# A fifth kind of expert for up to 32 tokens, and another order of the branches, in a two-layer decoder trunk

## The chip, the core and the metric

The kernel runs on one core of one Trainium2 chip. The metric is the device time of one execution in microseconds (us). The kernel before was timed three times; a profiled execution of it, with the trace that is read here, is a fourth. TensorE is PE in the rows (PEld its weight loads, PEldq and PEq its sequencer), VectorE is DVE, ScalarE ACT, GpSimd POOL, SyncE SP. MiB is 1,048,576 bytes.

## What is computed

The reference is two decoder layers on 256 tokens of 1024 channels. Only the last part matters here: in the second layer the channel mixer is a top-2-of-8 mixture of experts. Each expert is a SwiGLU with two 1024 x 2816 matrices and one 2816 x 1024 matrix in float32:

```python
def _moe(h, w_router, b_router, w1, w3, w2):
    t = h.reshape(-1, d)
    logits = (t @ w_router + b_router).astype(jnp.float32)
    top_val, top_idx = lax.top_k(logits, TOP_K)
    top_w = jax.nn.softmax(top_val, axis=-1)
    gates = jnp.sum(jax.nn.one_hot(top_idx, N_EXPERTS, dtype=jnp.float32) * top_w[..., None], axis=1)
    out = jnp.zeros_like(t)
    for e in range(N_EXPERTS):
        out = out + gates[:, e:e + 1].astype(t.dtype) * _swiglu(t, w1[e], w3[e], w2[e])
    return out.reshape(bsz, seq, d)
```

With the inputs that are timed, the reference sends 20, 54, 194, 113, 23, 40, 43 and 25 tokens to experts 0 to 7 (512 in all). The kernel computes only the tokens that an expert has.

## The kernel before, in words

Everything up to the router runs once in a fixed order. `moe` (L1098) then goes through the eight experts in order (L1417). The router counts each expert's tokens and turns the count into a number `ov` by three comparisons on DVE (L1049 to L1051): 0 for up to 64 tokens, 1 for up to 128, 2 for up to 208 (`MANY`), 3 above. For each expert all five engines load that number into a register (L1418) and take one of four bodies through nested branches (L1426 to L1435): `small` (L1168), `middle` (L1245), `many` with 208 slots, `many` with 256. In the program each branch is followed by the body of its true side, then by its false side; after a body the engine jumps to the point where the next expert's number is loaded. So `small` is entered without a jump, `middle` with one, `many` at 208 with two; and each body but the last one placed ends in a jump.

Weights. Each expert's weights are 33 parts of 1 MiB: 11 blocks, each of two parts of w1 and w3 (`w13m`) and one part of w2. They go through a ring of 15 buffers (L1091 to L1094), in one order for all eight experts (`parts`, L1085 to L1090), 264 parts in all. `refill` (L178) issues on SP every part that the ring has room for; the program calls it after each stage, and each issue waits on SP until PE has read the buffer's last part. `moe_begin` fills the ring once (L1095), during the end of the layer before.

`small` works on one 128 x 128 array of PE as two column groups of 64 columns (`tile_position=(0, 64 * h)`), each with the expert's 64 token slots as its stationary operand. It gathers the tokens from `hn` by a 0/1 matrix (L1175, the channels' halves in the two groups, 512 columns each), copies them out of PSUM on ACT and DVE (L1178, L1179), transposes them (L1183) and adds the shift (L1187). `stage1` (L1195) runs, for each block and each of 8 chunks of the contraction, one matmul per group over 256 columns of weights (L1200): w1's columns in the first group, w3's in the second. SiLU is on ACT (L1204), the product on DVE (L1205). `stage2` (L1208) transposes the product (L1212), copies it (L1215) and accumulates 512 columns of the output in each group (L1218). The groups' results are in two PSUM banks. The order is stage1(0), stage1(1), stage2(0), stage1(2), and so on; after the last block the rows are scaled (L1234), scattered back to the tokens by matmuls (L1240) and added to `x_t` on DVE (L1141). For the last expert each chunk of channels also goes through the final norm (`finish`, L1145), and four DMAs write the output (L1166).

A float32 matmul is two LDWEIGHTS and two MATMUL records in the trace; some records of a trace can be missing.

An expert of kind `middle` or `many` splits the weights into two parts on ACT and DVE (`load_parts`, L210 and L211) and multiplies with the whole array.

Of the kernel before, what the change touches and what calls it, by code (L numbers as in the profile page):

```python
# [9 lines left out]
F32 = mybir.dt.float32  # L10
# [4 lines left out]
AF = mybir.ActivationFunctionType  # L15
ALU = mybir.AluOpType
# [19 lines left out]
P = 128  # L36
D = 1024
KC = 8
T = 256
# [4 lines left out]
NB = 11  # L44
# [47 lines left out]
def trunk_kernel(ctx: ExitStack, tc: tile.TileContext, xT, sm, co, w_ada0, w_ada, w_in, w_v, s5bc, w_glu,  # L92
# [12 lines left out]
    def nm(s):  # L105
        cnt[0] += 1
        return f"{s}_{cnt[0]}"
# [990 lines left out]
    def moe():  # L1098
# [66 lines left out]
                for q in range(2):  # L1165
                    nc.sync.dma_start(out[tb * P:(tb + 1) * P, 512 * q:512 * q + 512], o[:, q, :])  # L1166

        def small(e):  # L1168

            pm = pms[e % 2]  # L1170
            hf = (slice(0, 64), slice(64, 128))
            ps = [mm_ps("xg") for _ in range(2)]
            for tb in range(2):
                for h in range(2):
                    PE.matmul(ps[h][hf[h], :], lhsT=pm[:, tb, 0:64], rhs=hn[:, tb, 512 * h:512 * h + 512],  # L1175
                              start=tb == 0, stop=tb == 1, tile_position=(0, 64 * h))
            xs = mo.tile([P, 512], F32, name=nm("xs"), tag="pt", bufs=2)
            S.activation(xs[hf[0]], ps[0][hf[0], :], AF.Copy)  # L1178
            V.tensor_copy(xs[hf[1]], ps[1][hf[1], :])  # L1179
            ps = mm_ps("xg")  # L1180
            xe = lp.tile([P, KC * 64], F32, name=nm("xs"), tag="hh")
            for c in range(4):
                PE.transpose(ps[:, c * P:(c + 1) * P], xs[:, c * P:(c + 1) * P], ident)  # L1183

            xe4, ps4 = (t.rearrange("p (c h s) -> p h c s", c=4, h=2) for t in (xe, ps))
            for h in range(2):
                V.tensor_tensor(xe4[:, h], ps4[:, h], sh[:, 4 * h:4 * h + 4].unsqueeze(2).broadcast_to([P, 4, 64]), op=ALU.add)  # L1187
            y = [ms_ps("y", 0) for _ in range(2)]

            def rows_of(src, rows, cols):  # L1190
                n = min(rows, 2048 // cols)
                return [w[:, r, :] for i in range(0, rows, n)
                        for w in (load_raw(src[:, i:i + n, :], n, cols),) for r in range(n)]

            def stage1(j):  # L1195
                w = rows_of(w13m[e, j], KC, 512)
                ps = [mm_ps("s1") for _ in range(2)]
                for k in range(KC):
                    for h in range(2):
# [3 lines left out]
                sg = mo.tile([P, 256], F32, name=nm("sg"), tag="pt", bufs=2)  # L1203
                S.activation(sg[hf[1]], ps[0][hf[0], 0:256], AF.Silu)  # L1204
                V.tensor_tensor(sg[hf[1]], sg[hf[1]], ps[1][hf[1], 0:256], op=ALU.mult)  # L1205
                return sg

            def stage2(j, sg):  # L1208
                w = rows_of(w2m[e, j], 2, 1024)
                ps = ms_ps("gT", 1)  # L1210
                for k in range(2):
                    PE.transpose(ps[:, k * 64:(k + 1) * 64], sg[hf[1], k * P:(k + 1) * P], ident[hf[1], hf[1]],  # L1212
                                 tile_position=(64, 0))
                g = mo.tile([P, 2, 64], F32, name=nm("gT"), tag="gT", bufs=2)
                S.activation(g, ps[:, 0:P].rearrange("p (k s) -> p k s", k=2), AF.Copy)  # L1215
                for k in range(2):
                    for h in range(2):
                        PE.matmul(y[h][hf[h], :], lhsT=g[:, k, :], rhs=w[k][:, 512 * h:512 * h + 512],  # L1218
                                  start=j == 0 and k == 0, stop=j == NB - 1 and k == 1, tile_position=(0, 64 * h))
                refill()  # L1220

            prev = None
            for j in range(NB):
                sg = stage1(j)
                if prev is not None:
                    stage2(j - 1, prev)
                prev = sg
                if j == 1:
                    ahead(e)
                    ge, gs = back_of(e, 64)  # L1230
            stage2(NB - 1, prev)
            ys = lp.tile([P, 512], F32, name=nm("ys"), tag="hh")
            for h in range(2):
                S.activation(ys[hf[h]], y[h][hf[h], :], AF.Copy, scale=gs[hf[h]])  # L1234
            gf = ge.bitcast(F32)
            fin.update(n=0, a=ms_ps)
            for c in range(4):
                ps = [mm_ps("sc") for _ in range(2)]
                for h in range(2):
                    PE.matmul(ps[h][:, 0:T], lhsT=ys[hf[h], c * P:(c + 1) * P], rhs=gf[hf[h], :],  # L1240
                              start=True, stop=True, tile_position=(64 * h, 0))
                for h in range(2):
                    add_back(e, 4 * h + c, ps[h][:, 0:T])

        def middle(e):  # L1245

# [168 lines left out]
                    add_back(e, 2 * q + i, ps[:, i * T:(i + 1) * T])  # L1415

        for e in range(NE):  # L1417
            rv = nc.values_load(ov[0:1, e:e + 1], engines=ENGS, min_val=0, max_val=3,  # L1418
                                skip_runtime_bounds_check_because="it is a sum of three comparisons")
# [194 lines left out]
```

## Time and profile before

| what | us |
|---|---|
| median of three runs | 1573.48 |
| lowest and highest of them | 1571.73 and 1580.18 |
| the profiled execution, its own time | 1569.24 |
| its span, first to last instruction | 1567.5 |
| experts 0 to 7 in it (from the first gather) | 744.7 to 1567.5 |

The span is what the trace shows, and all positions are counted from its start; 1.7 us of the execution's time lie around it. The first 744 us are the part that the change does not touch. In the experts' part the kinds follow one another as small, small, many (208), middle, small, small, small, small.

How to read it: the two engines that matter are PE and the DMA queue that brings the weights. Where the DMA share is 1 the 16 DMA engines are never idle and the weights set the pace; where it is well below, the ring is full and an engine sets the pace. A taken branch shows as a COMPARE_BRANCH record whose length is the time that the sequencer stood at it.

### The profile page before, as it was taken

How to read it: one execution, taken by the hardware profiler on the slowest of the kernel's cores; microseconds unless marked ns; L12 is line 12 of the kernel's file. 1: busy time of each engine (PE TensorE's matmuls, PEld its weight loads, DVE VectorE, ACT ScalarE, POOL GpSimd, SP SyncE). 2: the span in 40 equal slices, each digit the busy share in tenths (PEclk: the TensorE clock that was granted, in tenths of full speed). 3: DMA queues.
4: the chain of work that ended last, by engine and by line, in shares of the span. 5: the costliest groups of instructions: out<-in, count | busy, mean ns of one | idle time of the engine just before them, and what ended most of it. 6: DMA issues, size and time to landing. Idle time of an engine off the chain costs nothing.

```text
span 1567.5 us, 24755 instructions
## 1 busy us (share of the span) xinstructions
PE 1371.7 (88%) x9903; PEld 1139.8 (73%) x9903; DVE 881.6 (56%) x1443; ACT 605.2 (39%) x1115; POOL 318.9 (20%) x295
## 2 busy tenths in 40 slices
PE   4788999799998878988998949999799897979796
PEld 3676998699997777988665648988677574747474
DVE  7888679897777778687111036666588301010102
ACT  3453564354455534644111125555477211111112
POOL 0568019986201625050000000000000000000000
PEclk8898999799999899999998969999899998989899
DMA  7454356477776344479899975666399599999993
GB/s 285 174 190 160 125 188 212 136 258 240 261 257 223 133 136 135 166 244 403 359 419 416 419 290 189 215 203 203 130 348 351 212 420 416 419 416 419 417 419 122
DMA packets 60379, 420.37 MB, mean 268 GB/s; under 512 B 6688, under 2 KB 6688, under 8 KB 11296
## 3 DMA queue, kind: packets, MB, share of 16 engines
q1 hardware_dynamic: 56160, 403.34, 67.9%
q0 software_dynamic: 4032, 14.68, 2.8%
q8 instruction: 100, 1.64, 0.4%
q14 instruction: 87, 0.71, 0.1%
HBM read 416.94 MB, written 1.05 MB: 267 GB/s over the span
## 4 chain that ended last, share of the span: by engine, by line
PE 70%; DVE 18%; issue 6%; DMA 2%; ACT 2%; DVEq 0%; SPq 0%; ACTq 0%
PE s L1200 16%; PE mm L231 15%; PE y L1218 8%; DVE wl L211 6%; PE s L1350 4%; PE y L1372 4%; PE facc L971 3%; PE s L1267 3%; PE s L1352 2%; PE y L1286 2%; DMA raw<-in_w13m_dram 2%; DVE acc L309 1%; PE mm L716 1%; PE xg L1175 1%; DVE x_t L1141 1%
## 5 line engine op out<-in xcount | busy, mean ns | idle before, releaser
L211 DVE TENSOR_TENSOR wl<-raw,wh 128x1024 fp32r<-128x1024 f32 (+1 forms) x290 | 391.0, 1363 | 118.6 <-ACT wh L210 116.2
L210 ACT ACTIVATE wh<-raw 128x1024 fp32r<-128x1024 f32 (+1 forms) x290 | 302.3, 1057 | 252.1 <-PE mm L231 102.1
L231 PE MATMUL mm<-hh,wh 128*128 128x256 f32 x864 | 250.7, 292 | 5.1 <-ACT hh L250 2.9
L231 PE MATMUL mm<-hh,wl 128*128 128x256 f32 x864 | 249.7, 290 | 5.8 <-DVE wl L211 5.8
L1200 PE MATMUL s<-raw,xs 128*64 128x256 f32 x1920 | 250.1, 390 | 3.4 <-DVE xs L1187 3.4
L231 PE MATMUL mm<-hl,wh 128*128 128x256 f32 x864 | 249.5, 289 | 2.0 <-DVE hl L251 1.0
L1200 PEld LDWEIGHTS s<-raw,xs 128*64 128x64 f32 x1920 | 183.8, 140 | 48.2 <-issue 13.9
L1205 DVE TENSOR_TENSOR sg<-sg,s 64x256 f32<-64x256 f32 x66 | 28.0, 424 | 318.6 <-ACT sg L1204 269.8
L231 PEld LDWEIGHTS mm<-hh,wl 128*128 128x128 f32 x864 | 169.4, 196 | 9.8 <-DVE wl L211 6.3
L231 PEld LDWEIGHTS mm<-hh,wh 128*128 128x128 f32 x864 | 169.0, 196 | 9.4 <-ACT hh L250 3.3
L231 PEld LDWEIGHTS mm<-hl,wh 128*128 128x128 f32 x864 | 169.2, 196 | 3.7 <-DVE hl L409 1.5
L1218 PE MATMUL y<-raw,gT 128*64 128x512 f32 x520 | 143.1, 600 | 4.7 <-ACT gT L1215 4.7
L1204 ACT ACTIVATE sg<-s 64x256 f32<-64x256 f32 x66 | 24.8, 375 | 314.2 <-PE s L1200 314.2
L1350 PE MATMUL s<-xe,wh 128*128 128x416 f32 x352 | 107.2, 368 | 2.0 <-DVE sg L1360 1.7
L1352 PE MATMUL s<-xe,wl 128*128 128x208 f32 x352 | 91.0, 258 | 0.0
L309 DVE SCALAR_TENSOR_TENSOR acc<-raw,cond,acc 128x512 f32<-128x512 f32 x91 | 81.4, 894 | 1.6
L1218 PEld LDWEIGHTS y<-raw,gT 128*64 128x64 f32 x520 | 51.1, 136 | 40.9 <-issue 30.5
L317 POOL TENSOR_TENSOR araw<-araw,cond 128x1024 f32<-128x1024 f32 x28 | 62.3, 2229 | 71.8 <-DMA araw<-in_w_ada_dram 71.8
L1350 PEld LDWEIGHTS s<-xe,wh 128*128 128x128 f32 x352 | 66.2, 188 | 4.3 <-DVE sg L1360 2.4
L1352 PEld LDWEIGHTS s<-xe,wl 128*128 128x128 f32 x352 | 67.3, 191 | 0.4
L971 PE MATMUL facc<-fgh,wh 128*128 128x256 f32 x352 | 62.9, 281 | 0.2 <-ACT wh L210 0.2
L321 POOL TENSOR_TENSOR araw<-araw,araw 128x1024 f32<-128x1024 f32 x21 | 58.2, 2773 | 1.6
(513 smaller groups left out, 2369.0 us busy)
## 6 DMA issues: line engine op xcount, KB each, us to landing
raw<-in_w13m_dram SPq DMA_DIRECT2D x160, 1024.0 KB, 13.8
raw<-in_w2m_dram SPq DMA_DIRECT2D x87, 1024.0 KB, 13.7
raw<-in_w_ada_dram SPq DMA_DIRECT2D x32, 1024.0 KB, 5.1
raw<-in_w_in_dram SPq DMA_DIRECT2D x28, 1024.0 KB, 5.0
raw<-in_w13d_dram SPq DMA_DIRECT2D x22, 1024.0 KB, 5.0
late<-in_w13m_dram SPq DMA_DIRECT2D x16, 1024.0 KB, 16.2
araw<-in_w_ada_dram POOLq DMA_DIRECT2D x28, 512.0 KB, 4.6
raw<-in_w2d_dram SPq DMA_DIRECT2D x11, 1024.0 KB, 5.0
```

The costliest lines, as they stand in the source:

```text
L210: S.activation(hv, rv, AF.Copy)
L211: V.tensor_tensor(lv, rv, hv.bitcast(F32), op=ALU.subtract)
L231: PE.matmul(ps, lhsT=a[k][:, c0:c0 + P], rhs=b[:, k, :], start=k == 0 and i == 0 and o % 2 == 0, stop=k == n - 1 and i == 2 and o % 2 == 1)
L309: V.scalar_tensor_tensor(acc0, raw[:, k, :], c, acc0, op0=ALU.mult, op1=ALU.add)
L317: G.tensor_tensor(raw, raw, cond[:, r0:r0 + 2].unsqueeze(2).broadcast_to([P, 2, 512]), op=ALU.mult)
L321: G.tensor_tensor(acc, acc, raw, op=ALU.add)
L971: PE.matmul(o, lhsT=a[k][:, oc * P:(oc + 1) * P], rhs=b[:, k, :], start=j == 0 and oc % 2 == 0 and k == 0 and i == 0, stop=j == NB - 1 and ...
L1200: PE.matmul(ps[h][hf[h], 0:256], lhsT=xe4[:, k // 4, k % 4, :], rhs=w[k][:, 256 * h:256 * h + 256], start=k == 0, stop=k == KC - 1, tile_p ...
L1218: PE.matmul(y[h][hf[h], :], lhsT=g[:, k, :], rhs=w[k][:, 512 * h:512 * h + 512], start=j == 0 and k == 0, stop=j == NB - 1 and k == 1, til ...
L1350: PE.matmul(ps[:, 0:2 * nb], lhsT=hs[k][:, c], rhs=x.rearrange("p i s -> p (i s)"), start=k == 0, stop=False)
L1352: PE.matmul(ps[:, nb:2 * nb], lhsT=ls[k][:, c], rhs=x[:, 0, :], start=False, stop=k == KC - 1)
L1372: PE.matmul(y[b][n][0:s1 - s0, :], lhsT=g[:, k, s0:s1], rhs=w[w_][k][:, n * 512:n * 512 + 512], start=j == 0 and k == 0 and i == 0, stop=j ...
```

## The change

It adds a fifth kind. The comparison with 32 makes `ov` run from 0 to 4. `small(e, n)` now takes 32 or 64 slots: with n = 32 it uses four column groups of 32 columns (`G_ = 4`), each with a quarter of the weights' columns (128 in `stage1`, 256 in `stage2` and in the gather), so the number of matmuls doubles and each is half as wide. In both sizes the groups' results now lie in one PSUM bank instead of two, and the final scaling is one ACT instruction on 128 partitions instead of two on 64. The branches are nested anew, and three of them ask for the false side to be placed next (`preferred_fallthrough_block=False`).

```diff
-        V.tensor_scalar(o64, ps[:, 16:24], 64.0, None, op0=ALU.is_gt)
-        V.scalar_tensor_tensor(o64, ps[:, 16:24], float(P), o64, op0=ALU.is_gt, op1=ALU.add)
+        V.tensor_scalar(o64, ps[:, 16:24], 32.0, None, op0=ALU.is_gt)
+        for n in (64, P):
+            V.scalar_tensor_tensor(o64, ps[:, 16:24], float(n), o64, op0=ALU.is_gt, op1=ALU.add)
...
-        def small(e):
+        def small(e, n):
...
+            G_ = P // n
+            cb = KC // G_
+            gr = [slice(n * g, n * g + n) for g in range(G_)]
+            lo, hi = slice(0, 64), slice(64, 128)
+            w_ = D // G_
+            ps = mm_ps("xg")
             for tb in range(2):
...
+                for g in range(G_):
+                    PE.matmul(ps[gr[g], 0:w_], lhsT=pm[:, tb, 0:n], rhs=hn[:, tb, w_ * g:w_ * g + w_],
+                              start=tb == 0, stop=tb == 1, tile_position=(0, n * g))
...
-                ps = [mm_ps("s1") for _ in range(2)]
+                ps = mm_ps("s1")
+                c_ = 512 // G_
                 for k in range(KC):
-                    for h in range(2):
-                        PE.matmul(ps[h][hf[h], 0:256], lhsT=xe4[:, k // 4, k % 4, :], rhs=w[k][:, 256 * h:256 * h + 256],
-                                  start=k == 0, stop=k == KC - 1, tile_position=(0, 64 * h))
+                    for g in range(G_):
+                        PE.matmul(ps[gr[g], 0:c_], lhsT=xe4[:, k // cb, k % cb, :], rhs=w[k][:, c_ * g:c_ * g + c_],
+                                  start=k == 0, stop=k == KC - 1, tile_position=(0, n * g))
...
+                for k in range(2 * n // 64):
+                    PE.transpose(ps[:, k * 64:(k + 1) * 64], sg[hi, k * P:(k + 1) * P], ident[hi, hi], tile_position=(64, 0))
...
-                    for h in range(2):
-                        PE.matmul(y[h][hf[h], :], lhsT=g[:, k, :], rhs=w[k][:, 512 * h:512 * h + 512],
-                                  start=j == 0 and k == 0, stop=j == NB - 1 and k == 1, tile_position=(0, 64 * h))
+                    for h in range(G_):
+                        PE.matmul(y[gr[h], 0:w_], lhsT=g[:, k, :], rhs=w[k][:, w_ * h:w_ * h + w_],
+                                  start=j == 0 and k == 0, stop=j == NB - 1 and k == 1, tile_position=(0, n * h))
...
-            with tc.If(rv < 1) as c:
-                arm(small)
+
+            with tc.If(rv < 2, preferred_fallthrough_block=False) as c:
+                with tc.If(rv < 1, preferred_fallthrough_block=False) as c1:
+                    arm(lambda e: small(e, 32))
+                with c1.Else():
+                    arm(lambda e: small(e, 64))
             with c.Else():
-                with tc.If(rv < 2) as c2:
+                with tc.If(rv < 3, preferred_fallthrough_block=False) as c2:
                     arm(middle)
                 with c2.Else():
-                    with tc.If(rv < 3) as c3:
+                    with tc.If(rv < 4) as c3:
                         arm(lambda e: many(e, MANY))
```

Experts 0, 4 and 7 (20, 23 and 25 tokens) become the new kind; 1, 5 and 6 stay `small` with 64 slots.

## Rows read from the trace of the kernel before

**Rows 1.** The page's 40 slices of the span: DMA share and GB/s.

```profile
DMA  7454356477776344479899975666399599999993
GB/s 285 174 190 160 125 188 212 136 258 240 261 257 223 133 136 135 166 244 403 359 419 416 419 290 189 215 203 203 130 348 351 212 420 416 419 416 419 417 419 122
```

**Rows 2.** By stretch, experts 0, 2, 3, 6: length, busy per engine, PEclk, DMA share, GB/s.

```profile
726.00:827.00 101.00, 85.54 (x630) 60.73 (x628) 24.09 (x91) 18.51 (x49) 0.00 (x0) 0.93 0.96 396
...
909.00:1117.00 208.00, 183.45 (x1080) 164.66 (x1080) 122.49 (x185) 102.86 (x168) 0.00 (x0) 0.94 0.58 197
1117.00:1231.00 114.00, 106.88 (x474) 83.98 (x474) 91.65 (x102) 73.69 (x89) 0.00 (x0) 0.97 0.82 305
...
1394.00:1476.00 82.00, 72.75 (x506) 47.92 (x506) 10.12 (x25) 9.51 (x26) 0.00 (x0) 0.94 1.01 418
```

**Rows 3.** Short stretches: around expert 4's start, in expert 6, at the end.

```profile
1230.00:1240.00 10.00, 6.33 (x32) 2.72 (x34) 2.73 (x8) 0.59 (x1) 0.00 (x0) 0.83 0.01 2
...
1394.00:1400.00 6.00, 4.77 (x12) 1.57 (x12) 1.23 (x4) 0.59 (x1) 0.00 (x0) 0.50 1.01 410
...
1410.00:1420.00 10.00, 10.00 (x80) 6.91 (x78) 0.58 (x2) 1.03 (x3) 0.00 (x0) 1.00 1.01 421
...
1540.00:1542.00 2.00, 2.00 (x21) 1.86 (x19) 0.00 (x0) 0.00 (x0) 0.00 (x0) 1.00 0.04 16
```

**Rows 4.** Timeline of SP: first refill of expert 0, of expert 4, last weight issues.

```profile
754.81 0.33 SPq L183 DMA_DIRECT2D raw<-in_w13m_dram  x1
...
1239.96 0.33 SPq L183 DMA_DIRECT2D raw<-in_w13m_dram  x1
...
1519.55 2.81 SPq L183 DMA_DIRECT2D raw<-in_w2m_dram  x2
```

**Rows 5.** The chain in order of time: last stage2 and gathers (start, us, what).

```profile
815.34 1.99 PE y L1218 x8
...
827.38 3.70 PE xg L1175 x8
...
897.52 1.99 PE y L1218 x8
...
924.14 7.68 PE xg L1333 x48
...
1232.22 3.61 PE xg L1175 x8
...
1546.38 1.99 PE y L1218 x8
```

**Rows 6.** Branches by line and short stretch: ns min/median/max, first and last start.

```profile
L1426 PEldq COMPARE_BRANCH  x1: 95/95/95, 744.4 to 744.4; - x1
...
L1426 PEldq COMPARE_BRANCH  x2: 77/3108/6138, 820.5 to 827.1; - x2
...
L1426 PEldq COMPARE_BRANCH  x2: 5971/6575/7179, 902.7 to 909.1; - x2
...
L1429 PEldq COMPARE_BRANCH  x1: 7396/7396/7396, 916.5 to 916.5; - x1
...
L1426 PEldq COMPARE_BRANCH  x1: 4356/4356/4356, 1113.1 to 1113.1; - x1
...
L1429 PEldq COMPARE_BRANCH  x1: 3958/3958/3958, 1227.5 to 1227.5; - x1
...
L1426 SPq COMPARE_BRANCH  x2: 38/44/50, 906.7 to 907.5; - x2
...
L1429 SPq COMPARE_BRANCH  x1: 50/50/50, 912.2 to 912.2; - x1
```

**Rows 7.** Timeline of PE: four column groups (L282) and two (L1200).

```profile
28.80 1.07 PE L282 MATMUL adar<-raw,condr 128*32 128x256 f32 x16
...
1237.90 3.67 PE L1200 MATMUL s<-raw,xs 128*64 128x256 f32 x32 [0.57 <-DVE xs L1187]
```

**Rows 8.** Timeline of DVE in the router: one comparison of the counts.

```profile
743.15 0.17 DVE L1050 SCALAR_TENSOR_TENSOR rlg<-rank,rlg 128x8 f32<-128x8 f32 x1
```

More of the change, by code (lines that the diff above doesn't have):

```diff
@@ L1166, in finish @@
                     nc.sync.dma_start(out[tb * P:(tb + 1) * P, 512 * q:512 * q + 512], o[:, q, :])
-        def small(e):
+        def small(e, n):
             pm = pms[e % 2]
-            hf = (slice(0, 64), slice(64, 128))
-            ps = [mm_ps("xg") for _ in range(2)]
-            for tb in range(2):
-                for h in range(2):
[L1175 to L1179, printed above, removed]
+            G_ = P // n
[4 more added lines that the diff above has]
+            ps = mm_ps("xg")
+            for tb in range(2):
+                for g in range(G_):
+                    PE.matmul(ps[gr[g], 0:w_], lhsT=pm[:, tb, 0:n], rhs=hn[:, tb, w_ * g:w_ * g + w_],
+                              start=tb == 0, stop=tb == 1, tile_position=(0, n * g))
+            xs = mo.tile([P, w_], F32, name=nm("xs"), tag="pt", bufs=2)
+            S.activation(xs[lo], ps[lo, 0:w_], AF.Copy)
+            V.tensor_copy(xs[hi], ps[hi, 0:w_])
@@ L1180, in small @@
             ps = mm_ps("xg")
-            xe = lp.tile([P, KC * 64], F32, name=nm("xs"), tag="hh")
-            for c in range(4):
+            xe = lp.tile([P, KC * n], F32, name=nm("xe"), tag="hh")
+            for c in range(cb):
                 PE.transpose(ps[:, c * P:(c + 1) * P], xs[:, c * P:(c + 1) * P], ident)
-            xe4, ps4 = (t.rearrange("p (c h s) -> p h c s", c=4, h=2) for t in (xe, ps))
-            for h in range(2):
-                V.tensor_tensor(xe4[:, h], ps4[:, h], sh[:, 4 * h:4 * h + 4].unsqueeze(2).broadcast_to([P, 4, 64]), op=ALU.add)
@@ L1188, in small @@
-            y = [ms_ps("y", 0) for _ in range(2)]
+            xe4, ps4 = (t[:, 0:KC * n].rearrange("p (c g s) -> p g c s", c=cb, g=G_) for t in (xe, ps))
+            for g in range(G_):
+                V.tensor_tensor(xe4[:, g], ps4[:, g], sh[:, cb * g:cb * g + cb].unsqueeze(2).broadcast_to([P, cb, n]),
+                                op=ALU.add)
+            y = ms_ps("y", 0)
             def rows_of(src, rows, cols):
-                n = min(rows, 2048 // cols)
-                return [w[:, r, :] for i in range(0, rows, n)
-                        for w in (load_raw(src[:, i:i + n, :], n, cols),) for r in range(n)]
+                m = min(rows, 2048 // cols)
+                return [w[:, r, :] for i in range(0, rows, m)
+                        for w in (load_raw(src[:, i:i + m, :], m, cols),) for r in range(m)]
@@ L1195, in stage1 @@
             def stage1(j):
                 w = rows_of(w13m[e, j], KC, 512)
-                ps = [mm_ps("s1") for _ in range(2)]
+                ps = mm_ps("s1")
+                c_ = 512 // G_
                 for k in range(KC):
-                    for h in range(2):
-                        PE.matmul(ps[h][hf[h], 0:256], lhsT=xe4[:, k // 4, k % 4, :], rhs=w[k][:, 256 * h:256 * h + 256],
-                                  start=k == 0, stop=k == KC - 1, tile_position=(0, 64 * h))
+                    for g in range(G_):
+                        PE.matmul(ps[gr[g], 0:c_], lhsT=xe4[:, k // cb, k % cb, :], rhs=w[k][:, c_ * g:c_ * g + c_],
+                                  start=k == 0, stop=k == KC - 1, tile_position=(0, n * g))
@@ L1210, in stage2 @@
                 ps = ms_ps("gT", 1)
+                for k in range(2 * n // 64):
+                    PE.transpose(ps[:, k * 64:(k + 1) * 64], sg[hi, k * P:(k + 1) * P], ident[hi, hi], tile_position=(64, 0))
+                g = mo.tile([P, 2, n], F32, name=nm("gT"), tag="gT", bufs=2)
+                S.activation(g, ps[:, 0:2 * n].rearrange("p (k s) -> p k s", k=2), AF.Copy)
                 for k in range(2):
[L1212 to L1217, printed above, removed]
-                        PE.matmul(y[h][hf[h], :], lhsT=g[:, k, :], rhs=w[k][:, 512 * h:512 * h + 512],
-                                  start=j == 0 and k == 0, stop=j == NB - 1 and k == 1, tile_position=(0, 64 * h))
+                    for h in range(G_):
+                        PE.matmul(y[gr[h], 0:w_], lhsT=g[:, k, :], rhs=w[k][:, w_ * h:w_ * h + w_],
+                                  start=j == 0 and k == 0, stop=j == NB - 1 and k == 1, tile_position=(0, n * h))
                 refill()
@@ L1229, in small @@
                     ahead(e)
-                    ge, gs = back_of(e, 64)
+                    ge, gs = back_of(e, n)
             stage2(NB - 1, prev)
-            ys = lp.tile([P, 512], F32, name=nm("ys"), tag="hh")
-            for h in range(2):
-                S.activation(ys[hf[h]], y[h][hf[h], :], AF.Copy, scale=gs[hf[h]])
+            ys = lp.tile([P, w_], F32, name=nm("ys"), tag="hh")
+            S.activation(ys, y[:, 0:w_], AF.Copy, scale=gs)
             gf = ge.bitcast(F32)
             fin.update(n=0, a=ms_ps)
[L1237 to L1243, printed above, removed]
+            for c in range(cb):
+                ps = [mm_ps("sc") for _ in range(G_)]
+                for g in range(G_):
+                    PE.matmul(ps[g][:, 0:T], lhsT=ys[gr[g], c * P:(c + 1) * P], rhs=gf[gr[g], :],
+                              start=True, stop=True, tile_position=(n * g, 0))
+                for g in range(G_):
+                    add_back(e, cb * g + c, ps[g][:, 0:T])
         def middle(e):
@@ L1417, in moe @@
         for e in range(NE):
-            rv = nc.values_load(ov[0:1, e:e + 1], engines=ENGS, min_val=0, max_val=3,
-                                skip_runtime_bounds_check_because="it is a sum of three comparisons")
+            rv = nc.values_load(ov[0:1, e:e + 1], engines=ENGS, min_val=0, max_val=4,
+                                skip_runtime_bounds_check_because="it is a sum of four comparisons")
             def arm(f):
```

6 lines of the change are left out of this document (3 added, 3 removed).

## The prediction

> **What bounds the kernel now.** First the page's slices: the DMA share stands at 9 from slice 18 to 23 and again near the end, at 400 to 420 GB/s [rows 1]. Only the experts' part is changed, so the second view is one row per expert. Expert 6 (64 slots) holds the DMA engines at share 1.01 and 418 GB/s for all of its 82 us; expert 0 is at 0.96; expert 2 (208 slots) at 0.58 and expert 3 (128 slots) at 0.82 are bound by PE and the engines that feed it [rows 2]. At 418 GB/s a part of 1 MiB takes 2.51 us, an expert's 33 parts 82.8 us: as long as PE spends on a small expert. Both limits lie on one another, and a faster PE alone can gain only what the ring has in stock.
>
> So I count when the DMA queue stops and starts. It starts again with the first refill of an expert that found the ring full: 754.8 in expert 0, 1240.0 in expert 4 [rows 4]; just before the latter the share is 0.01 [rows 3]. From 1240.0, experts 4 to 7 need 132 - 15 = 117 more parts, 293.7 us; the last bytes come at about 1541.5 [rows 3], 301.5 us after the first refill, since the engines finish unevenly. PE ends its last stage2 at 1546.38 + 1.99 = 1548.4 [rows 5], 19.1 us before the end.
>
> The third view is the branches [rows 6]. One not taken costs PE under 0.1 us. One taken with the weight queue busy costs 5.97 to 7.40 us, with the queue idle 3.96 to 4.36. Between experts 1 and 2 PE takes three: the exit and two on the way to `many`.
>
> **The change, step by step.** I call the branches A (rv < 2), B (rv < 1), C (rv < 3). With the false side next, `many` at 208 is entered without a jump, `middle` by C, `small` with 64 by A, with 32 by A and B. The body with 32 lies last, so I give it no exit jump; the others keep theirs. For a taken branch I use 7.0 us with the queue busy (entries 7.18 and 7.40, exits nearer 6) and 4.2 idle [rows 6].
>
> *Matmuls.* Four groups of 32 columns run in the trace already: 16 records of 256 columns in 1.07 us, four steps; two groups of 64 take 3.67 us for 32 records, 16 steps [rows 7]. The 12 steps between them are 2.60 us, 0.217 each, and a tail of 0.4 is left: four records side by side cost what two cost. At 128 columns I take half a step, 0.108. A block of the new body then needs 16 x 0.108 + 4 x 0.217 = 2.6 us of matmuls and about 0.5 around them, against 16 x 0.217 + 4 x 0.43 + 0.5 = 5.7 before. The DMA queue needs 7.5 us per block. The new body waits for weights once the ring is empty.
>
> *Expert 0.* The extra comparison is 0.2 us [rows 8]. PE's branch at 744.4 was not taken [rows 6]; now A and B are, +14.0 (bounds: 8.4 if the ring has filled by then, 14.8). In return gather, transposes and the first part of stage1 are half as long, about 4 us of the 10.4 between branch and first refill (bounds 0 and 5.5). First refill 754.8 + 0.2 + 14 - 4 = 765. The queue is idle until then, so this is paid in full. The expert's last part is 18 refills later: 765 + 45.2 + 2.5 (landing) + 1.5 = 814 for the end of its stage2, against 815.34 + 1.99 = 817.3 [rows 5].
>
> *Expert 1.* Before, 3.2 us lay between that end and the branch at 820.5, and 6.9 to the gather at 827.4, of which 6.1 was the exit branch [rows 5, 6]. Now: 814 + 3.2 + 0.7 + 7.1 (A taken, B not) = 825.0. Its PE time, gather to last stage2, was 899.5 - 827.4 = 72.1 [rows 5], so 897.1; by the weights it is 765 + 51 x 2.51 + 4.5 = 897.5. I take 897.5: 2 us ahead.
>
> *Expert 2.* Two taken branches (7.18 + 7.40) become two not taken, -14.4 [rows 6]. Its gather, at 924.1 before [rows 5], comes 16 us ahead. Experts 2 and 3 stay PE-bound [rows 2], and between them one entry is taken as before: still 16.
>
> *Expert 4.* The way in had no jump; now A and B with the queue idle, +8.4 (14.8 if they cost what they do under load). Its gather (1232.2 before [rows 5]) is 7.6 ahead; half the gather and half the first stage1 part save another 3.4 of the 7.7 us to the first refill (bounds 0 and 4). First refill 1229, 11 us ahead.
>
> *Experts 4 to 7.* The queue needs the same 301.5 us, if it never stops. It stops if PE enters expert 7 too late. From 1229, by the same steps: expert 4 ends its stage2 at 49.2, expert 5 at 132.5, expert 6 at 149.6 + 72.1 = 221.7; then 3.2 + 0.7 + 6.1 (exit) + 14 (A, B) and 4.3 to the first refill give 250. The ring then holds work for the queue up to 99 x 2.51 + 2.5 = 251. With a microsecond or two until new bytes flow I count 1.5 us idle (bounds 0 and 6). SP takes the same branches, 4.7 us for one (907.5 to 912.2 [rows 6]); it is covered, since the last weights issued at about 1522 [rows 4] land 20 us later, and that much is in flight when SP jumps. POOL has no work in an expert. ACT and DVE branch beside PE, and I count PE.
>
> *The end.* Last bytes at 1229 + 301.5 + 1.5 = 1532; PE has then only the last stage2 to do, 1.5 us with its copy, where before it ended 6.9 after the last bytes. One scaling instruction instead of two saves 0.7 of the last 19.1 us: 1532 + 1.5 + 18.4 = 1551.9.
>
> The sum is -15.6 us on the span: of it -2 in experts 0 and 1, -14.4 before expert 2, +8.4 - 3.4 at expert 4, -4.6 at the end, rounded. The profiled execution's own 1569.24 becomes 1553.6. It was 4.2 us under the median of the runs; from the median 1573.48 I come to **1558**.
>
> [...]
>
> [...]
>
> **The rivals.**
>
> *Branches dearer than seen* (slower). The new body has about twice the PE instructions, and a taken branch into it may cost more than any row. Each extra microsecond counts three times before expert 1's end (A, B, A) and four times before expert 7's first refill (A, A, A, B), once the 1.5 us of slack there are gone. At 12 us per branch: -15.6 + 15 + 20 = +19, 1593. It passes +0.5% from about 10.4 us. Against it: no row is above 7.40.
>
> *The gain is eaten* (no difference). 7.4 at every entry, no quicker first refills (the copies and additions around the half-length matmuls are not halved) and 6 us of idle queue at expert 7: -15.6 + 4.8 + 3.4 + 4.5 = -2.9, 1571.
>
> *The order of the branches does not change.* Then 32 slots enter without a jump and `many` keeps two. Expert 0 refills at 754.8 and ends at 804, expert 1 at 893 (6 ahead), expert 4 refills 9.8 ahead, and the end falls at 1551.6 of the span: 1558, the same number by another way.
>
> *One PSUM bank serialises the groups* (slower). Then 64 slots lose 5.2 us a block, 57 an expert; three experts, some of it inside the weights' time: about 1710. The four-group row writes one bank and runs at 0.217 a step [rows 7].
>
> *PE was the bound.* If PE's 2.6 us per block came off fully, 3 experts x 11 x 2.6 = 85: 1488. The DMA share of 1.01 [rows 2] forbids it.
>
> [...]
>
> **How the numbers follow.** About 0.5%, or 8 us, is what a measurement here can tell from no change. The forecast has 0.58, the order unchanged 0.05, PE as the bound 0.01: faster 0.64. Eaten gain 0.25: same 0.25. Dearer branches 0.09 and serialised groups 0.02: slower 0.11. The range: 8.4 for expert 0's entry, no idle at expert 7 and the best refills give 1549; above it takes in the eaten gain with the clock's 1.4 and a little more, 1574. What is left out are the dear branches, the bank and PE as the bound.
>
> **What would show it.** Right: A and B as two long records at expert 0, the DMA share down to zero between about 757 and 765; expert 2's gather near 908; expert 4's first refill near 1229; PE waiting for weights in experts 0, 4 and 7; the last bytes near 1532 and the end 20 us later. Wrong: a taken branch over 10 us; the two-group matmuls no longer 0.217 a step; PE not waiting for weights with 32 slots; a long idle stretch of the queue before expert 7; a jump on the way to `many`.

## The result, and the profile after

The changed kernel takes 1582.44 us (median of 20 runs, 1575.28 to 1596.67), the kernel before 1571.93 (20 runs, 1564.14 to 1583.3). The ratio is 1.0072, with a 95% interval of 1.005 to 1.0094: the change made the kernel slower by 0.7%. I had predicted 1558 and faster; 1582 lies above the range too.

The profiled execution has a span of 1579.8 us against 1567.5. First the page's slices, which answer to [rows 1]:

```profile
PEclk9798999899998999999768989999899788989796
DMA  7454455477775434569699995655598499999993
GB/s 291 165 198 148 134 185 202 147 260 243 273 256 197 161 103 152 184 227 415 270 417 414 419 367 201 213 202 172 189 355 338 169 418 412 419 405 420 392 373 154
```

The queue is full in the same parts as before. What differs is when it starts and stops. PE's branches (rows of one line and stretch: engine, count, ns min/median/max, first and last start), which answer to [rows 6]:

```profile
L1433 PEldq COMPARE_BRANCH  x1: 6142/6142/6142, 746.3 to 746.3; - x1
L1434 PEldq COMPARE_BRANCH  x1: 4772/4772/4772, 752.5 to 752.5; - x1
...
L1434 PEldq COMPARE_BRANCH  x1: 5910/5910/5910, 820.3 to 820.3; - x1
...
L1433 PEldq COMPARE_BRANCH  x1: 7127/7127/7127, 826.7 to 826.7; - x1
...
L1439 PEldq COMPARE_BRANCH  x1: 3427/3427/3427, 1226.3 to 1226.3; - x1
...
L1434 PEldq COMPARE_BRANCH  x1: 6066/6066/6066, 1299.9 to 1299.9; - x1
...
L1434 PEldq COMPARE_BRANCH  x2: 6267/6928/7588, 1476.1 to 1489.8; - x2
```

Expert 0 is entered by A and B, 10.9 us together. The third row is one that the prediction does not have: the body with 32 slots is left at 820.3 by a jump of 5.91 us, and at 1299.9 (expert 4) by one of 6.07. The body with 128 slots too is left by a jump, at 1226.3 (expert 3), and so is the one with 208, at 1107.4 for 3.49 us. The last row holds two at expert 7: the exit of expert 6 and the entry by B. Only PE's records have the length of the wait: on DVE a branch that is taken has a record as short as one that is not (47 ns for its jump out of expert 1, 43 for the first at expert 2, which is not taken), and the wait stands behind it.

The first refills on SP of experts 0, 4 and 7 (start, length), which answer to [rows 4]:

```profile
765.39 0.33 SPq L183 DMA_DIRECT2D raw<-in_w13m_dram  x1
...
1246.66 0.33 SPq L183 DMA_DIRECT2D raw<-in_w13m_dram  x1
...
1504.18 0.33 SPq L183 DMA_DIRECT2D raw<-in_w13m_dram  x1
```

Before, they were at 754.81 and 1239.96. Short stretches (length, busy per engine with counts, PEclk, DMA share, GB/s), which answer to [rows 3]:

```profile
756.00:765.00 9.00, 5.02 (x60) 3.15 (x61) 4.45 (x28) 1.66 (x2) 0.00 (x0) 0.50 0.01 3
1228.00:1240.00 12.00, 0.00 (x0) 0.00 (x0) 1.99 (x6) 0.00 (x0) 0.00 (x0) 0.64 0.06 10
1495.00:1507.00 12.00, 8.26 (x151) 6.08 (x151) 1.34 (x6) 0.65 (x2) 0.00 (x0) 0.60 0.60 225
...
1545.00:1557.00 12.00, 7.68 (x114) 4.13 (x114) 0.58 (x2) 0.98 (x4) 0.00 (x0) 0.78 0.60 247
1560.00:1570.00 10.00, 9.75 (x30) 5.36 (x30) 4.80 (x12) 5.83 (x16) 0.00 (x0) 0.50 0.00 1
```

The queue is idle before expert 0's first refill, as predicted, and again around expert 7's, with a share of 0.60 over 12 us. At the end PE is granted 0.50. In the kernel before, the stretch behind the last stage2 was at 1.00:

```profile
1548.00:1558.00 10.00, 8.08 (x42) 4.85 (x40) 6.13 (x17) 7.44 (x18) 0.00 (x0) 1.00 0.01 2
```

In the chain in order of time, the rows that answer to [rows 5]:

```profile
794.52 20.11 DMA raw<-in_w2m_dram
...
814.76 1.99 PE y L1225 x16
...
834.09 1.94 PE xg L1180 x3
...
1535.48 19.88 DMA raw<-in_w2m_dram
...
1555.49 1.83 PE y L1225 x16
```

Expert 0 now waits for weights: its last stage2 starts 0.1 us after a transfer has landed. It ends at 816.7 instead of 817.3, but expert 1's gather comes at 834.1 instead of 827.4. The gap between was 10.1 us and is 17.3. The last transfer lands at 1555.4 (before 1541.9; its last bytes were there at 1541.5), and from the end of the last stage2 to the end of the span there are 22.5 us instead of 19.1.

At expert 2, PE takes no jump, as predicted, and starts its gather at 916.5. There it stops. The timelines of DVE and of PE (start, busy time, line, operation; in brackets the idle time before it and what ended it):

```profile
916.70 0.48 DVE L1120 TENSOR_SCALAR pm<-co_t,rrk 128x128 f32<-128x128 f32 x2 [5.49 <-issue]
917.09 0.16 DVE L1329 TENSOR_SCALAR r<-rrk 128x2 f32<-128x2 f32 x1
921.44 0.48 DVE L1332 TENSOR_SCALAR pml<-co_t,r 128x128 f32<-128x128 f32 x2 [4.18 <-issue]
```

```profile
916.52 1.20 PE L1339 MATMUL xg<-pm,late 128*128 128x128 f32 x4 [6.13 <-issue]
921.78 1.15 PE L1339 MATMUL xg<-pml,late 128*128 128x80 f32 x4 [4.06 <-DVE pml L1332]
```

The second block of the gather needs `pml`, which DVE makes at 921.4, after 4.18 us in which it waited for nothing that the profile shows, behind its own jump out of expert 1's body. So the gather goes on at 921.8; before it began at 924.1.

### The profile page after: what moved, and what is told of

It reads as the page before. It is cut to its first block, busy times and chain, and to the rows that moved or that the text cites. A ratio compares the mean times of both kernels' runs of the same rounds, so it can differ in the third digit from the quotient of the medians.

```text
span 1579.8 us, 27425 instructions
## 1 busy us (share of the span) xinstructions
PE 1309.9 (83%) x11256; PEld 1113.0 (70%) x11256; DVE 875.8 (55%) x1450; ACT 595.2 (38%) x1109; POOL 318.4 (20%) x295
## 4 chain that ended last, share of the span: by engine, by line
PE 62%; DVE 17%; issue 9%; DMA 8%; ACT 2%; DVEq 0%; ACTq 0%; SPq 0%
PE mm L231 15%; PE s L1207 10%; PE y L1225 5%; DVE wl L211 5%; PE s L1356 4%; PE y L1378 4%; PE facc L971 3%; DMA raw<-in_w13m_dram 3%; PE s L1273 3%; DMA raw<-in_w2m_dram 3%; PE s L1358 2%; PE y L1292 2%; DVE acc L309 2%; PE mm L716 1%; DMA late<-in_w2m_dram 1%
## 5 line engine op out<-in xcount | busy, mean ns | idle before, releaser
L211 DVE TENSOR_TENSOR wl<-raw,wh 128x1024 fp32r<-128x1024 f32 (+1 forms) x290 | 387.0, 1348 | 120.0 <-ACT wh L210 117.4
L1207 PE MATMUL s<-raw,xe 128*32 128x128 f32 (+1 forms) x2880 | 202.8, 326 | 15.8 <-DMA raw<-in_w13m_dram 12.4
L1207 PEld LDWEIGHTS s<-raw,xe 128*32 128x32 f32 (+1 forms) x2880 | 158.3, 124 | 43.9 <-DMA raw<-in_w13m_dram 17.1
L1212 DVE TENSOR_TENSOR sg<-sg,s 64x128 f32<-64x128 f32 (+1 forms) x66 | 23.6, 358 | 294.3 <-ACT sg L1211 294.3
L1211 ACT ACTIVATE sg<-s 64x128 f32<-64x128 f32 (+1 forms) x66 | 21.3, 323 | 269.8 <-PE s L1207 269.8
L1225 PE MATMUL y<-raw,gT 128*32 128x256 f32 (+1 forms) x776 | 112.9, 488 | 8.9 <-DMA raw<-in_w2m_dram 4.2
L1180 PE MATMUL xg<-late,pm 128*32 128x256 f32 (+1 forms) x72 | 16.5, 770 | 84.9 <-issue 84.9
L1225 PEld LDWEIGHTS y<-raw,gT 128*32 128x32 f32 (+1 forms) x776 | 44.6, 124 | 36.6 <-issue 13.0
L1180 PEld LDWEIGHTS xg<-late,pm 128*32 128x32 f32 (+1 forms) x72 | 4.6, 178 | 92.0 <-issue 92.0
L1358 PEld LDWEIGHTS s<-xe,wl 128*128 128x128 f32 x352 | 67.2, 191 | 0.4
## 6 DMA issues: line engine op xcount, KB each, us to landing
raw<-in_w2m_dram SPq DMA_DIRECT2D x87, 1024.0 KB, 18.7
```

Source lines behind the costliest of these rows:

```text
L211: V.tensor_tensor(lv, rv, hv.bitcast(F32), op=ALU.subtract)
L1207: PE.matmul(ps[gr[g], 0:c_], lhsT=xe4[:, k // cb, k % cb, :], rhs=w[k][:, c_ * g:c_ * g + c_], start=k == 0, stop=k == KC - 1, tile_positi ...
L1225: PE.matmul(y[gr[h], 0:w_], lhsT=g[:, k, :], rhs=w[k][:, w_ * h:w_ * h + w_], start=j == 0 and k == 0, stop=j == NB - 1 and k == 1, tile_p ...
L1358: PE.matmul(ps[:, nb:2 * nb], lhsT=ls[k][:, c], rhs=x[:, 0, :], start=False, stop=k == KC - 1)
```

## The experiments

My theory after the result (J in the expectations) was that the jumps decide: the body with 32 slots is a gain, and the entries and above all its exit cost more than it brings. The rivals were that four column groups cost more than they bring (G), that a program of five bodies is slower to fetch in any order (F), and, for the end alone, that the starved PE falls to half clock (H) or that the work behind this body does so by itself (T).

The part ahead of the router is the same in all these kernels, but its length differs by execution: PE's first branch starts between 740 and 757 us in the profiled ones (744.4 before, 746.3 after), with a granted clock of 0.85 to 0.95 in the stretch from 600 to 700 us. So I give positions **from that branch** as well: the kernel before ends at 823.0 by it, the changed one at 833.4.

**The body taken out, the branches kept**

```diff
-                    arm(lambda e: small(e, 32))
+                    arm(lambda e: small(e, 64))
```

> The changed kernel with one thing undone: up to 32 tokens go through the same five-way branches into the same place, but the body there works with 64 slots on two column groups. Theory J (the loss is PE's taken branches, and the new body itself is a gain): expert 0 refills first near 769, its last stage2 ends near 832, expert 1 gathers near 849 and expert 2 near 936. From expert 4's gather near 1255 four bodies of 72.4 and gaps of 17.3, 17.3 and 24.5 give 1604 for the last stage2 and 1623 for the span, a ratio of 1.035 to the kernel before. Rival G (the body with four groups is what costs: it starves and its end is at half clock): no slower than the changed kernel, 1.000 to 1.007, and the part after the last stage2 is 19 us again instead of 22.5.

Measured: ratio 1.035 (1.0321 to 1.0378). Expert 0's last stage2 ends at 837.7, expert 1 gathers at 854.8 and expert 4 at 1260.1 in an execution whose first branch is 7.6 us later than in the changed kernel; the end is 873.9 from the branch. Rival G falls: behind the new branches four column groups are worth 40 us. The time behind the last stage2 is 18.7 us here, so 3.8 us of the 22.5 do come with the body.

**The order of the branches as before, with the new body**

```diff
-            with tc.If(rv < 2, preferred_fallthrough_block=False) as c:
-                with tc.If(rv < 1, preferred_fallthrough_block=False) as c1:
+            with tc.If(rv < 2) as c:
+                with tc.If(rv < 1) as c1:
...
-                with tc.If(rv < 3, preferred_fallthrough_block=False) as c2:
+                with tc.If(rv < 3) as c2:
```

> The changed kernel with the branches led as in the kernel before: the body with 32 slots is entered without a jump, 64 with one, 128 with one, 208 with two. Theory J: expert 0 refills first near 753, its last stage2 ends near 804, expert 1 gathers at 822, expert 2 at 919, expert 4 at 1227 with its first refill at 1234. Expert 7 is entered in time (no idle stretch of the DMA queue), last bytes at 1535, last stage2 at 1538, span 1560: ratio 0.995. Rival G (the body costs more than it brings): 1.000 to 1.01. Rival F (a program with five bodies is slower to fetch, whatever its order): 1.005 to 1.01, with expert 1's gather no earlier than 827.

Measured: 1.0004 (0.998 to 1.0029), no difference; I had expected 0.995. In its trace the end is 817.1 from the branch, 5.9 before that of the kernel before, where 7.5 was expected; expert 2's gather is at 171.9 (before 179.7). The medians show less than the trace, and the part ahead of the router can differ by that much. F, which wanted expert 1's gather no earlier than 827, has it at 825.9 in an execution that reached the branch 5.2 us late: it falls.

**As that, but 208 slots ahead of 128** (the edit against the run just above)

```diff
-                with tc.If(rv < 3) as c2:
+                with tc.If(rv < 3, preferred_fallthrough_block=False) as c2:
```

> As the light-first order, but 208 slots are placed ahead of 128: 32 slots without a jump, 64 with one, 208 with one, 128 with two. Theory J: as the light-first kernel up to expert 1; expert 2's gather near 911 (up to 916 if DVE waits again for its code), expert 3 near 1109, expert 4 near 1223, last bytes near 1532, span 1557: ratio 0.993. If DVE's wait before expert 2's second block eats the jump that is saved, no better than the light-first kernel, 0.995 to 0.997. Rivals G and F as there: 1.000 or more.

Measured: 0.9962 (0.9939 to 0.9984). J's 0.993 lies outside that; by its time the run falls where a wait on DVE was to eat the jump that is saved (0.995 to 0.997), but its trace has no such wait: expert 2 gathers at 912.7 without a stop. The end is 814.7 from the branch. One jump less at expert 2 and one more at expert 3 are worth 2.4 us in the traces.

**The prediction's world: 32 slots placed last**

```diff
+            with tc.If(rv > 1) as c:
+                with tc.If(rv > 2) as c2:
                     with tc.If(rv < 4) as c3:
                         arm(lambda e: many(e, MANY))
...
+                with c2.Else():
+                    arm(middle)
+            with c.Else():
+                with tc.If(rv > 0) as c1:
+                    arm(lambda e: small(e, 64))
+                with c1.Else():
+                    arm(lambda e: small(e, 32))
```

Here and in the next run the diff shows added lines and their surroundings alone.

> The same number of taken branches into every body as in the changed kernel, but the body with 32 slots now stands last, so that the jump behind it leads to the instruction next to it. It is the world that the prediction assumed. If a jump costs by what it skips: the exits of experts 0 and 4 take under 1 us instead of 5.9 and 6.1, expert 1 gathers near 828, expert 2 near 916, expert 4 refills first at 1241, the DMA queue is idle some 3 us at expert 7 instead of 6.5, span 1570, ratio 1.001. If any taken branch costs the same wherever it leads: exits of 5.9 as before, ratio 1.007.

Measured: 0.9991 (0.9969 to 1.0012); by the medians' ratios the new place gives back 0.8%, all that the change had lost. Its rows at the same places (PE's branch into expert 1, and its exit from there; DVE at the start of expert 2; SP's first refills of experts 4 and 7):

```profile
L1433 PEldq COMPARE_BRANCH  x1: 5956/5956/5956, 824.4 to 824.4; - x1
...
L1442 PEldq COMPARE_BRANCH  x1: 6032/6032/6032, 909.8 to 909.8; - x1
```

```profile
908.06 3.22 DVE L1142 SCALAR_TENSOR_TENSOR x_t<-sc,ada,x_t 128x256 f32<-128x256 f32 x8 [6.01 <-PE sc L1246]
911.34 0.48 DVE L1120 TENSOR_SCALAR pm<-co_t,rrk 128x128 f32<-128x128 f32 x2
911.74 0.16 DVE L1329 TENSOR_SCALAR r<-rrk 128x2 f32<-128x2 f32 x1
911.94 0.48 DVE L1332 TENSOR_SCALAR pml<-co_t,r 128x128 f32<-128x128 f32 x2
```

```profile
1240.42 0.34 SPq L183 DMA_DIRECT2D raw<-in_w13m_dram  x1
...
1499.72 0.33 SPq L183 DMA_DIRECT2D raw<-in_w13m_dram  x1
```

Between expert 0's last stage2 (820.9) and that branch there is no exit record any more, and the gap to expert 1's gather is 9.8 us instead of 17.3. The second gain I had not foreseen: DVE goes from expert 1's last addition to expert 2's `pm` in under 0.1 us, where it stood idle for 5.49 us in the changed kernel, and `pml` follows at once. The 64-slot body's exit now skips only the short 32-slot body. Expert 2's gather is at 164.6 from the branch instead of 175.5 (taken where it goes on), expert 4's at 481.7 instead of 493.8, the end at 820.3 instead of 833.4. Of these 13.1 us 5.8 are there at the end of expert 1's last stage2 (the gap's 7.5 and 1.7 in expert 0, less 3.4 for which expert 1 now waits for weights), 5.1 more come from DVE, and the rest are small; 1.1 of them lie behind the last stage2 (21.4 us instead of 22.5), where expert 7 has no exit jump either. One expectation failed: the queue was to be idle 3 us at expert 7. Its first refill there comes 259.3 us after expert 4's (changed kernel 257.5), and from expert 4's first refill to the last landing it is 308.8 us, as long as in the changed kernel, although expert 4 has no exit jump here and expert 5 gathers 62.6 us after that refill instead of 67.2.

**All heavy kinds first, one jump for every light one**

```diff
+            with tc.If(rv > 0) as c:
+                with tc.If(rv > 1) as c1:
+                    with tc.If(rv > 2) as c2:
...
+                    with c2.Else():
+                        arm(middle)
                 with c1.Else():
                     arm(lambda e: small(e, 64))
             with c.Else():
...
+                arm(lambda e: small(e, 32))
```

> All five kinds in one chain of branches with the heavy kinds first and 32 slots last: 208 is entered without a jump, each other kind with one, and the body with 32 slots leaves by a jump to the instruction next to it. Counted from the first branch after the router (before: expert 2's gather at 179.7, expert 4's at 487.8, the end at 823.0; the run with 32 slots last: 164.6, 481.7, 820.3). Theory J (PE's jumps over other bodies are what the change pays): one jump of 6 less than that run at expert 0, one of 4.7 less at expert 4: expert 2's gather at 159, expert 4's at 472, the DMA queue idle at expert 7 by 0 to 1 us instead of 2.5, end at 807: ratio 0.990. If the queue's rate from expert 4 on, not the jumps, set the end of the better orders, no better than the mixed order: 0.996.

Measured: 1555.85 us, ratio 0.9887 (0.9844 to 0.9929); the end is 805.6 from the branch, 17.5 before that of the kernel before. Every step came within 2.5 us of where J had it: gathers at 161.5 and 474.4, and the first refills of experts 4 and 7 are 251.0 apart (SP's timeline):

```profile
1232.76 0.34 SPq L183 DMA_DIRECT2D raw<-in_w13m_dram  x1
...
1483.74 0.34 SPq L183 DMA_DIRECT2D raw<-in_w13m_dram  x1
```

The ring had stock for about that long, so the queue hardly stopped: the last transfer landed 302.1 us after the first of these rows (308.7 in the changed kernel, 302.0 in the kernel before). Against the run above, expert 7 is entered by one jump instead of two: 16.9 us from expert 6's last stage2 to its gather instead of 24.5. This version beats both kernels.

**The same order without the fifth kind**

```diff
-                    with tc.If(rv > 2) as c2:
-                        with tc.If(rv < 4) as c3:
+                    with tc.If(rv < 3) as c2:
...
-                    with c2.Else():
-                        arm(middle)
                 with c1.Else():
-                    arm(lambda e: small(e, 64))
+                    arm(middle)
             with c.Else():
-                arm(lambda e: small(e, 32))
+                arm(lambda e: small(e, 64))
```

This diff is against the chain; the router has the comparisons of the kernel before, and 64 slots stay in one PSUM bank.

> The change without its fifth kind: no body with 32 slots, 64 slots in one PSUM bank, and the chain of branches with the heavy kinds first and 64 slots last (entered by one jump, left by a jump to the next instruction). Theory J: expert 0 enters 6 later and is bound by PE, expert 1 loses 7 and gains 6, expert 2 gains the exit of 6 and two entries of 14.6, so its gather is near 166 from the first branch (before 179.7), expert 4's near 478 (before 487.8), and at most 1 us is lost at each later expert, so that PE ends its last stage2 6 us earlier than before: ratio 0.996. The difference to the chain of five kinds (0.990) is then what 32 slots on four column groups bring by themselves: 0.006. If they bring nothing in this order either, both are equal.

Measured: 0.9926 (0.9897 to 0.9956), better than expected; the end is 808.9 from the branch. So the order, put so that the body that is used most lies last, gives some 0.7% (with the one PSUM bank and the one scaling instruction, which this run keeps; the body with 64 slots is no faster by them, 72.4 us in the changed kernel and 72.1 before). The 32 slots add 3.3 us by the traces, and 0.4% by the ratios, whose intervals overlap. Four column groups are a small gain here because the weights set the pace from expert 4 on (DMA share 1.01 from 1497 to 1527 in the chain), and because of the end: counted from the branch the last stage2 ends 7.4 us earlier with them (784.2 against 791.6), but 21.4 us follow it instead of 17.3.

**PE kept busy at the end: 16, 8 and 4 extra matmuls**

The lines stand in `stage1`, ahead of its matmuls; in two more kernels 8 and 4 take the place of 16.

```diff
+                if n == 32 and e == NE - 1 and j >= 6:
+                    for _ in range(16):
+                        PE.matmul(ps[:, 384:512], lhsT=ident, rhs=ident, start=True, stop=True)
```

> The chain of branches, and in expert 7's body with 32 slots 16 more matmuls of 128 columns ahead of each stage1 from block 6 on, into unused columns of its PSUM tile, so that PE has work while it waits for weights. Theory H (the end is 3.4 us longer because PE, starved, is at half clock when the last bytes come): the granted clock in the last 50 us is 1.00, the part after the last stage2 is 18.5 us instead of 21.4, ratio 0.988. If the clock at the end has another cause, the same part stays at 21 to 22.5 us and the ratio at the chain's 0.990 or above it, by what the extra matmuls delay.

> The changed kernel with the same extra matmuls in expert 7 alone. Theory H: the part after the last stage2 is 19.2 us instead of 22.5 and the last stage2 itself 1.1 us instead of 1.8, so 4 us less: ratio 1.0045 against 1.0072. Otherwise 1.007 or more.

> The chain of branches with 8 extra matmuls ahead of each of expert 7's last five stage1 instead of 16. With 16 PE ended its last stage2 7.0 us after the last bytes (chain without them: 1.7), so half the dose, 1.7 us per block, should leave PE starved and no later: last stage2 within 2 us of the last bytes. Theory H (busy PE before the end keeps the clock after it): the part after the last stage2 is 18 to 19 us instead of 21.4, ratio 0.987. Rival T (the scatter and norm behind a body with 32 slots fall to half clock by themselves, whatever ran before): 20.5 to 21.4 us as with 16, ratio 0.989.

> As the run with 8, with 4 extra matmuls ahead of each of expert 7's last five stage1. Theory H: the granted clock before the last stage2 is between that of the chain without them (0.62 and 0.84 in its last two stretches of 10 us) and 1.00, and the part after it between 18 and 21.4 us. Rival T: 21 to 21.4 us. Ratio 0.988 to 0.990 by either.

Measured: 0.9922 (0.9888 to 0.9956) for 16 in the chain, 1.0101 (1.0066 to 1.0136) for 16 in the changed kernel, 0.9904 (0.9869 to 0.9939) and 0.9911 (0.9879 to 0.9943) for 8 and 4 in the chain. None beats the chain by its median, so as a remedy it failed. The traces tell more. Two stretches of 10 us, around the last bytes and after them, for the chain, then for 16, then for 8 extra matmuls (columns as above):

```profile
1527.00:1537.00 10.00, 6.05 (x105) 3.65 (x105) 0.29 (x1) 0.97 (x3) 0.00 (x0) 0.84 0.52 214
1537.00:1547.00 10.00, 9.19 (x29) 4.08 (x25) 5.68 (x14) 5.56 (x15) 0.00 (x0) 0.50 0.00 0
```

```profile
1539.00:1549.00 10.00, 9.03 (x146) 6.60 (x144) 0.50 (x2) 1.02 (x5) 0.00 (x0) 1.00 0.03 11
1549.00:1559.00 10.00, 8.68 (x29) 4.13 (x30) 5.69 (x14) 5.90 (x17) 0.00 (x0) 0.62 0.00 0
```

```profile
1527.00:1537.00 10.00, 5.94 (x98) 3.68 (x97) 0.29 (x1) 0.72 (x3) 0.00 (x0) 0.83 0.56 230
1537.00:1547.00 10.00, 7.86 (x45) 3.84 (x45) 5.53 (x14) 5.84 (x16) 0.00 (x0) 0.83 0.00 0
```

With 16, PE was no longer starved but late: the last bytes came at 1541.7, the last stage2 ended at 1548.7. It was granted 1.00 from 1539 to 1549 and lost it in the scatter all the same: 0.62 from 1549 to 1559, where a scatter matmul pair at 1552.2, 2.8 us after the first, takes 1.15 us. The time behind the last stage2 is 20.6 us; in the changed kernel with 16 the granted clock falls from 1.00 (1557 to 1567) to 0.71 (1567 to 1577). With 8 it was 1.6 us behind the last bytes and kept 0.83 in the stretch after: 18.8 us instead of 21.4, and an end at 803.2 instead of 805.6. With 4 the stretch from 1540 to 1550, after the last bytes, was granted 0.50, as in the chain. In the row for 8 a scatter matmul pair takes 0.62 us at first and 1.15 after the fall, which is what the time consists of:

```profile
1539.25 0.75 PE sc L1249 x8
...
1541.81 0.62 PE sc L1249 x2
...
1542.81 0.62 PE sc L1249 x2
...
1543.82 1.15 PE sc L1249 x2
```

So the 3 to 4 us at the end are a matter of the clock; that starving alone takes it is not shown, since with 16 it fell without starving. Nor is it shown that the 8 extra matmuls held it: ahead of the last bytes the rows of the chain and of this run are alike (granted 0.84 and 0.83, PE busy for 6.05 and 5.94 us), and each is one execution. What would hold the clock through the scatter stays open, and no version with extra matmuls is measurably better than the chain.

## Why the prediction was wrong

The loss came in by two steps. The first is the sentence "The body with 32 lies last, so I give it no exit jump". That a body in the last place leaves without a jump was right; the run with that body really last has no record there. But with the false sides placed first the body with 32 slots does not lie last: all four kinds that are used leave by a jump, so that only the body with 256 slots, which no expert takes, can stand behind the others (whether 128 slots lie in between too no trace shows). Its exit costs 5.91 and 6.07 us, like the exits in [rows 6]. The second is a cover: "ACT and DVE branch beside PE, and I count PE".

Counted from the branch, the changed kernel ends 26 us later than predicted. The run with 32 slots last, which has neither that exit nor the wait on DVE, gives back the whole loss, 13.1 us of the 26. It does not bring the gain: it is 0.9991 and still 13 us late. The other half lies in terms that were mis-sized, at expert 4, in the queue's stop at expert 7 and at the end. In the order of the sum (measured positions are shifted by the 1.9 us that this execution reached the router later):

*Expert 0's entry and refill: right, by two errors that cancel.* A and B were taken at 14.0 and took 10.9; the queue ran dry during B (DMA share 0.39 from 752 to 756). Half-length gather and stage1 were to save 4 and saved 2.2: from the gather to the first refill 7.9 us instead of 10.1. The refill came at 763.5; predicted 765.

*Expert 1: 7 late.* Predicted gather 825.0, measured 832.2: the exit. Predicted end 897.5, measured 904.5.

*Expert 2: 12 late.* The two jumps that go, 14.4 us, did go on PE. But PE was not alone there. DVE's jump out of expert 1 and the stop behind it made `pml` late, 5.3 us after PE was ready. The run with 32 slots last shows it by removing it.

*Expert 4's first refill: 16 late.* The entry cost 9.75 (8.4 counted), and the quicker first refill saved 1.2 us, not 3.4: 6.5 us between gather and refill instead of 7.7. The time around the half-length matmuls is not halved, as the rival of the eaten gain had it.

*Expert 7: its refill 23 late, the last bytes 21.* I put its first refill 250 us after expert 4's, 1 us inside the ring's stock, and counted 1.5 us idle. It came after 257.5. From expert 4's first refill to the last landing it was 308.7 us instead of the 302.0 before: 6.7 us lost where 1.5 were counted, and more than the bound of 6. The step that failed is not the exit, though it put expert 5's gather at 67.2 us after the refill. It is the 132.5 for the end of expert 5: in the changed kernel that was 138.1, but it was also 137.2 in the run with 32 slots last and 137.5 in the chain, which have no exit from expert 4. Part 51, expert 5's last, was taken to land 130.5 us after the first refill and the stage2 to end 2.0 later; in these two runs it landed after 133.8 and 132.4, and the stage2 ended 3.4 and 5.1 us behind it. Another 2.3 us are expert 7's first refill, 6.6 us after its gather where 4.3 were counted. What cures the stop is one entry jump less, as the chain shows.

*The end: 26 late.* I counted 18.4 us behind the last stage2, and it was 22.5: the scatter and the norm's transposes ran at a granted clock of 0.50 (1560 to 1570), with 1.15 us for a scatter pair (0.63 in the kernel before, at 1.00). The 1.4 us that the range counts for the clock are my estimate, and no run shows them: the last stage2 took 1.83 us in the changed kernel and 1.13 in the chain, and what the low clock lengthened was the part behind it. What the granted clock follows is not shown. By the profile's busy time, behind the last stage2 the changed kernel's PE is busy for 9.75 of 10 us at 0.50, the kernel before's for 8.08 of 10 at 1.00; with 16 extra matmuls in the chain, PE is busy for 9.03 of 10 us at 1.00 around the end of the last stage2, and the next 10 are granted 0.62. The starved body itself was granted 0.85 from 1535 to 1545, busy for 5.50 of 10.

With the 1.9 us ahead of the router the sum of these is 28: 1579.8 instead of 1551.9.

What was right: four records of 32 columns side by side in one bank cost no more than foreseen (32 records in 1.08 us), the two-group body keeps its pace (72.4 us from gather to last stage2, 72.1 before), the queue and not PE sets the end, and PE's jumps cost about what the rows had (4.8 to 7.6 us beside the weights, 3.4 to 5.0 around experts 3 and 4). Of the rivals "the gain is eaten" was nearest: it had the idle queue at expert 7 and the slower refills. "Branches dearer than seen" had the right sign and a wrong reason: not a dearer jump, but an exit that I had not counted and a jump on another engine.

## What to carry to other kernels

Count the jumps of a branched program from its built order, entry and exit of every body and on every engine, before a body's saving is counted; on PE an exit was free only behind the body that is placed last (behind the others it took 3.4 to 6.3 us in the changed kernel), so the body that is used most, or whose followers are on the critical path, belongs there. Where engine and queue run at the same pace, a shorter body is worth only what the queue lost before it: here, in single traces, 32 slots gave 3 us in the best order, and the order itself 14. A time that a ring's stock covers by 1 us is not covered.

## What was not expected of the hardware

In the run with 32 slots last, PE leaves that body without a record and without any time that shows; whether the program holds a jump there, no trace says. And what a jump costs differs by engine and by place. Out of the 64-slot body, over the 32-slot one, PE needs 6.03 us and DVE shows under 0.1 of idle time (its last addition ends at 911.28, `pm` starts at 911.34); in the changed kernel, where at least the body with 256 slots lies on the way as well, DVE stood 5.49 us. The body that is skipped is long on PE and short on DVE (the run with 32 slots last, expert 0's body: length, then busy and instructions of PE, PEld, DVE, ACT and POOL):

```profile
758.80:821.40 62.60, 45.31 (x941) 32.08 (x941) 7.80 (x40) 7.85 (x26) 0.00 (x0) 0.85 0.83 334
```

A short body is not always skipped for nothing: behind its jump B of the changed kernel DVE stood 4.65 us in expert 0, and 0.2 in expert 4 (branch at 1234.3, `pm` at 1234.5).

Why a taken branch holds the engine is not shown; on PE it held it for 3.4 to 7.6 us here. The trace has DMA packets of the kind `instruction` at some of these places: during the exit from expert 0 of the changed kernel, one of 16 KiB starts at 823.7, on queue q8. They start without a jump near them too (on q8 at 1263.9, 1270.2 and 1276.4, inside expert 4's body). DVE's second stop, 4.18 us a few instructions behind its jump, has nothing in the profile's semaphores to wait for, but three such packets start in it: one of 16 KiB on q8 (918.9) and two of 8 KiB on q14 (919.1 and 919.5). That DVE waits for the next piece of its code there is my guess; which queue serves which engine the trace does not say, and no run tried it.
